# The first token and all weights in one DMA queue: reordering the start of a top-2 mixture-of-experts combine

## The chip, the core and the metric

The kernel runs on one core of a Trainium2 chip. The metric is the device time of one execution in microseconds (us), the median of three runs. The engines that matter here are VectorE (DVE in the profile), ScalarE (ACT), SyncE (SP), which computes nothing and issues transfers, and the core's 16 DMA engines, which move all data between device memory (DRAM) and the on-chip memory (SBUF, 128 partitions). SyncE and ScalarE each have a queue of their own for transfers; in the profile q1 is SyncE's and q10 is ScalarE's.

## The reference

```python
batch, seq, hidden, n_experts, k = 16, 1024, 512, 8, 2
# expert_outputs:  (16, 1024, 2, 512) float32
# combine_weights: (16, 1024, 2)      float32
def reference(expert_outputs, combine_weights):
    weights = combine_weights[..., np.newaxis]
    return np.sum(expert_outputs * weights, axis=2).astype(np.float32)
```

For each of the 16384 tokens two expert vectors of 512 elements are scaled by two weights and added. In float32 the input is 67.1 MB, the weights are 0.13 MB and the output is 33.6 MB, so 100.8 MB cross between DRAM and SBUF. There are two multiplications and an addition for every output element, and no matmul.

## The kernel before

A token here is a row of 2 x 512 float32 numbers, 4 KB long. Each of the 128 partitions handles 128 tokens: 120 in ten tiles of 12 tokens and 8 in a last, smaller tile. A full tile is 128 partitions x 48 KB, 6.29 MB. Four buffers hold tiles.

```python
J, LAST = 12, 8
main = per - LAST          # 120 tokens per partition in full tiles
...
ipool = ctx.enter_context(tc.tile_pool(name="in", bufs=4))
wt = wpool.tile([P, per * k], dt)

for t, c in ((0, main), (main, LAST)):          # weights: two DMAs in ScalarE's queue
    nc.scalar.dma_start(
        out=wt[:, k * t : k * (t + c)].rearrange("p (t k) -> p t k", k=k), in_=cw(t, c)
    )
warm = wpool.tile([P, 1], dt)
nc.scalar.activation(out=warm, in_=..., func=copy)
```

The two weight transfers have rows of 960 B and of 64 B per partition. The first serves the ten full tiles, the second the last tile only. The activation called `warm` loads ScalarE's function table early.

```python
for g in range(last + 1):
    et = ipool.tile([P, J, k * h], dt)
    ot = ...                                     # the first half of et, reused for the result
    t0, c = g * J, J if g < last else LAST

    for a, m in ((0, 2), (2, c - 2)) if g == 0 else ((0, c),):
        nc.sync.dma_start(
            out=et[:, a : a + m], in_=eo(t0 + a, m),
            max_dma_last_dim=k * h * 4 if g + a == 0 else None,
        )
    if g < last - 1:                             # tiles 0 to 8: VectorE alone
        ...
        nc.vector.tensor_tensor(out=ek, in0=ek, in1=wb, op=mult)                          # L78
        nc.vector.tensor_tensor(out=ot, in0=et[:, :, 0:h], in1=et[:, :, h : 2 * h], op=add)  # L79
        nc.scalar.dma_start(out=o(t0, c), in_=ot)
        continue
    ...                                          # tiles 9 and 10: ScalarE scales one half, VectorE does the rest
    nc.sync.dma_start(out=o(t0, c), in_=ot[:, 0:c])
```

The load of tile 0 is in two pieces: the first two tokens in rows of 4 KB (1024 KB in all), and then the other ten (5120 KB, rows of 40 KB). Every other tile is one load. VectorE's first multiply (L78) works on the whole of tile 0 at once. Loads stand in SyncE's queue; the stores of tiles 0 to 8 stand in ScalarE's, those of tiles 9 and 10 in SyncE's. A load into a buffer that was used before waits until the store from it has finished, so from tile 4 on loads and stores follow one another.

Of the kernel before, what the change touches and what calls it, by code (L numbers as in the profile page):

```python
# [1 line left out]

# [4 lines left out]


@with_exitstack
def kernel(  # L10
    ctx: ExitStack,
    tc: tile.TileContext,
    expert_outputs: bass.AP,
    combine_weights: bass.AP,
    out: bass.AP,
):

    nc = tc.nc  # L20
    b, s, k, h = expert_outputs.shape
    assert k == 2
    n = b * s
    P = nc.NUM_PARTITIONS
    per = n // P
    assert per * P == n
    J, LAST = 12, 8
    main = per - LAST
    assert main % J == 0
    eo = expert_outputs.rearrange("b s k h -> (b s) (k h)")  # L30
    cw = combine_weights.rearrange("b s k -> (b s) k")
    o = out.rearrange("b s h -> (b s) h")

    def rows(x):

        a = x[0 : P * main, :].rearrange("(p t) f -> p t f", p=P)
        b = x[P * main : n, :].rearrange("(p t) f -> p t f", p=P)
        return lambda t, c: a[:, t : t + c, :] if t < main else b[:, t - main : t - main + c, :]

    eo, cw, o = rows(eo), rows(cw), rows(o)  # L40

    dt = mybir.dt.float32
    mult = mybir.AluOpType.mult
    add = mybir.AluOpType.add
    copy = mybir.ActivationFunctionType.Copy

    last = main // J

    wpool = ctx.enter_context(tc.tile_pool(name="w", bufs=1))
    ipool = ctx.enter_context(tc.tile_pool(name="in", bufs=4))  # L50

    wt = wpool.tile([P, per * k], dt)

    for t, c in ((0, main), (main, LAST)):
        nc.scalar.dma_start(
            out=wt[:, k * t : k * (t + c)].rearrange("p (t k) -> p t k", k=k), in_=cw(t, c)
        )

    warm = wpool.tile([P, 1], dt)
    nc.scalar.activation(out=warm, in_=nc.const_aps.tensor(1.0, (P, 1), dt), func=copy)  # L60

    for g in range(last + 1):
        et = ipool.tile([P, J, k * h], dt)

        ot = et.rearrange("p j f -> p (j f)")[:, 0 : J * h].rearrange("p (j f) -> p j f", f=h)
        t0, c = g * J, J if g < last else LAST

        for a, m in ((0, 2), (2, c - 2)) if g == 0 else ((0, c),):
            nc.sync.dma_start(  # L69
                out=et[:, a : a + m],  # L70
                in_=eo(t0 + a, m),
                max_dma_last_dim=k * h * 4 if g + a == 0 else None,
            )
        if g < last - 1:

            wb = wt[:, g * J * k : (g + 1) * J * k].unsqueeze(2).to_broadcast([P, J * k, h])
            ek = et.rearrange("p j (k h) -> p (j k) h", k=k)
# [6 lines that stand above are left out]
        for i in range(c):  # L84
            t = t0 + i
            nc.scalar.activation(  # L86
                out=et[:, i, 0:h], in_=et[:, i, 0:h], func=copy, scale=wt[:, 2 * t : 2 * t + 1]
            )
            if g == last:
                nc.vector.scalar_tensor_tensor(  # L90
                    out=ot[:, i, :],
                    in0=et[:, i, h : 2 * h],
                    scalar=wt[:, 2 * t + 1 : 2 * t + 2],
                    in1=et[:, i, 0:h],
                    op0=mult,
                    op1=add,
                )
        if g < last:
            w1 = wt.rearrange("p (t k) -> p t k", k=k)[:, t0 : t0 + c, 1:2]
            x1 = et[:, :, h : 2 * h]  # L100
            nc.vector.tensor_tensor(out=x1, in0=x1, in1=w1.to_broadcast([P, c, h]), op=mult)  # L101
            nc.vector.tensor_tensor(out=ot, in0=et[:, :, 0:h], in1=x1, op=add)  # L102
        nc.sync.dma_start(out=o(t0, c), in_=ot[:, 0:c])


# [1 line left out]
_INS = ['expert_outputs', 'combine_weights']  # L107
_OUTS = [((16, 1024, 512), 'float32')]


# [23 lines left out]
```

## Time and profile before

| Quantity | Before |
|---|---|
| Device time, median of 3 runs | 239.06 us (238.92 to 240.28) |
| Span of the profiled execution | 237.3 us |
| VectorE busy | 193.9 us, 28 instructions |
| ScalarE busy | 14.0 us, 22 instructions |
| DRAM read, written | 67.24 MB, 33.55 MB |
| Multiply of one tile on VectorE | 12.96 us |
| Addition of one tile on VectorE | 6.56 us |
| Load of a full tile, issue to landing (median) | 29.9 us |
| Store of a full tile through ScalarE's queue, issue to landing (median) | 32.7 us |

The span is measured by the profiler on the core and is a little shorter than the device time. "Issue to landing" counts from the moment at which an engine issues a transfer until its completion is signalled; much of it is time in which the transfer shares the DMA engines with others or stands behind them. A line such as L78 is a line of the kernel's source. In the list of groups, the last part of a row tells how long the engine stood idle just before instructions of this group, and what ended the wait.

### The profile page before, as it was taken

Reading aid. Unit: us, or ns where it says so; the run is one execution under the profiler, and the core shown is the slowest. Engines: PE = TensorE matmul, PEld = TensorE weight load, DVE = VectorE, ACT = ScalarE, POOL = GpSimd, SP = SyncE. Lnnn points to the kernel's source line nnn. Section 1 sums busy time; section 2 is a strip of 40 time slices with the busy share of each in tenths; the row PEclk is TensorE's granted clock in tenths of the full one; section 3 lists DMA queues with packets and bytes.
Section 4 is the critical chain, followed back from the end, with each engine's and each line's share of the span. In section 5 each row is a group of like instructions: output and inputs, shape, how many; then the busy total and the mean of one; then the engine's idle time right before and its main releaser. Section 6 shows DMA issues by size and latency. Waiting matters only on the chain.

```text
span 237.3 us, 154 instructions
## 1 busy us (share of the span) xinstructions
DVE 193.9 (82%) x28; ACT 14.0 (6%) x22; POOL 0.2 (0%) x4
## 2 busy tenths in 40 slices
DVE  0008999999999999999999879969996998785710
ACT  2000000000000000000000000000000000740800
POOL 0000000000000000000000000000000000000000
DMA  8999999989899999999897999999997979999997
GB/s 308 443 456 406 398 431 497 398 356 505 356 439 435 427 464 464 398 398 522 348 522 344 452 427 435 464 464 398 398 522 340 530 336 460 458 403 442 402 438 309
DMA packets 3728, 100.80 MB, mean 425 GB/s; under 512 B 528, under 2 KB 656, under 8 KB 912
## 3 DMA queue, kind: packets, MB, share of 16 engines
q1 hardware_dynamic: 2144, 72.35, 71.1%
q10 hardware_dynamic: 1584, 28.44, 27.9%
HBM read 67.24 MB, written 33.55 MB: 425 GB/s over the span
## 4 chain that ended last, share of the span: by engine, by line
DMA 59%; DVE 33%; ACT 2%; DVEq 0%; ACTq 0%; issue 0%; SPq 0%
DMA et<-in_expert_outputs_dram 30%; DMA out_dram<-et 29%; DVE et L78 22%; DVE et L79 11%; ACT et L86 2%; DVE et L90 1%; DVEq L129 0%; ACTq L129 0%; SPq L69 0%; DVEq L78 0%; ACTq L86 0%
## 5 line engine op out<-in xcount | busy, mean ns | idle before, releaser
L78 DVE TENSOR_TENSOR et<-et,wt 128x12288 f32<-128x12288 f32 x9 | 116.6, 12955 | 25.2 <-DMA et<-in_expert_outputs_dram 25.2
L79 DVE TENSOR_TENSOR et<-et 128x6144 f32<-128x6144 f32 x9 | 59.0, 6558 | 0.3
L86 ACT ACTIVATE et<-et,wt 128x512 f32<-128x512 f32 x20 | 12.5, 707 | 209.2 <-DMA et<-in_expert_outputs_dram 209.2
L90 DVE SCALAR_TENSOR_TENSOR et<-et,wt 128x512 f32<-128x512 f32 x8 | 5.6, 748 | 3.9 <-ACT et L86 3.7
L101 DVE TENSOR_TENSOR et<-et,wt 128x6144 f32<-128x6144 f32 x1 | 6.6, 6559 | 2.3 <-DMA et<-in_expert_outputs_dram 2.3
L102 DVE TENSOR_TENSOR et<-et 128x6144 f32<-128x6144 f32 x1 | 6.6, 6559 | 0.9 <-ACT et L86 0.9
L60 ACT ACT_TABLE_LOAD x1 | 1.3, 1283 | 1.7 <-issue 1.7
L60 ACT ACTIVATE warm<-const-float32-1.0 128x1 f32<-128x1 f32 x1 | 0.2, 202 | 0.0
L118 POOL MEMSET const-bfloat16-1.0<- 128x1 bf16 x1 | 0.1, 102 | 0.0
L118 POOL MEMSET const-uint8-127<- 128x1 uint8 x1 | 0.1, 102 | 0.0
L118 POOL MEMSET const-float32-0.0<- 128x1 f32 x1 | 0.1, 99 | 0.2 <-issue 0.2
L118 POOL MEMSET const-float32-1.0<- 128x1 f32 x1 | 0.1, 99 | 0.0
## 6 DMA issues: line engine op xcount, KB each, us to landing
et<-in_expert_outputs_dram SPq DMA_DIRECT2D x9, 6144.0 KB, 29.9
out_dram<-et ACTq DMA_DIRECT2D x9, 3072.0 KB, 32.7
et<-in_expert_outputs_dram SPq DMA_DIRECT2D x1, 5120.0 KB, 17.3
et<-in_expert_outputs_dram SPq DMA_DIRECT2D x1, 4096.0 KB, 25.1
out_dram<-et SPq DMA_DIRECT2D x1, 3072.0 KB, 14.6
out_dram<-et SPq DMA_DIRECT2D x1, 2048.0 KB, 10.0
et<-in_expert_outputs_dram SPq DMA_DIRECT2D x1, 1024.0 KB, 5.4
wt<-in_combine_weights_dram ACTq DMA_DIRECT2D x1, 120.0 KB, 4.4
```

The costliest lines, as they stand in the source:

```text
L60: nc.scalar.activation(out=warm, in_=nc.const_aps.tensor(1.0, (P, 1), dt), func=copy)
L78: nc.vector.tensor_tensor(out=ek, in0=ek, in1=wb, op=mult)
L79: nc.vector.tensor_tensor(out=ot, in0=et[:, :, 0:h], in1=et[:, :, h : 2 * h], op=add)
L86: nc.scalar.activation(out=et[:, i, 0:h], in_=et[:, i, 0:h], func=copy, scale=wt[:, 2 * t : 2 * t + 1])
L90: nc.vector.scalar_tensor_tensor(out=ot[:, i, :], in0=et[:, i, h : 2 * h], scalar=wt[:, 2 * t + 1 : 2 * t + 2], in1=et[:, i, 0:h], op0=mul ...
L101: nc.vector.tensor_tensor(out=x1, in0=x1, in1=w1.to_broadcast([P, c, h]), op=mult)
L102: nc.vector.tensor_tensor(out=ot, in0=et[:, :, 0:h], in1=x1, op=add)
L118: nc = _bacc.Bacc("TRN2", target_bir_lowering=False, num_devices=1)
```

## The change

The start is rearranged, and nothing else is. Before, the weights were issued by ScalarE while SyncE issued the first two tokens as one transfer and then the rest of tile 0. After, SyncE issues all of them, one behind another in one queue: the first token, the weights of the full tiles, the weights of the last tile, the second token, and the other ten tokens of tile 0. Each of the two single tokens is one DMA with rows of 4 KB per partition, so the option that cut rows to 4 KB isn't needed any more.

The aim is an orderly start: a large transfer is first in line, the small weight rows come right behind it, and none of them takes turns with tile data from another queue. ScalarE issues no load any more, and its `warm` activation stands at the head of its program.

```diff
-    for t, c in ((0, main), (main, LAST)):
-        nc.scalar.dma_start(
+    warm = wpool.tile([P, 1], dt)
+    nc.scalar.activation(out=warm, in_=nc.const_aps.tensor(1.0, (P, 1), dt), func=copy)
+
+    def load_weights(t, c):
+        nc.sync.dma_start(
             out=wt[:, k * t : k * (t + c)].rearrange("p (t k) -> p t k", k=k), in_=cw(t, c)
         )
-
-    warm = wpool.tile([P, 1], dt)
-    nc.scalar.activation(out=warm, in_=nc.const_aps.tensor(1.0, (P, 1), dt), func=copy)
 
     for g in range(last + 1):
         ...
+        if g == 0:
 
-        for a, m in ((0, 2), (2, c - 2)) if g == 0 else ((0, c),):
-            nc.sync.dma_start(
-                out=et[:, a : a + m],
-                in_=eo(t0 + a, m),
-                max_dma_last_dim=k * h * 4 if g + a == 0 else None,
-            )
+            nc.sync.dma_start(out=et[:, 0:1], in_=eo(0, 1))
+            load_weights(0, main)
+            load_weights(main, LAST)
+            nc.sync.dma_start(out=et[:, 1:2], in_=eo(1, 1))
+        a = 2 if g == 0 else 0
+        nc.sync.dma_start(out=et[:, a:c], in_=eo(t0 + a, c - a))
```

## The prediction, made before the changed kernel had run

> **What bounds the kernel now.** I read the profile from the whole to the detail: the span in slices with the queue table under it, the chain that ended last, the groups of instructions, then the DMA issues and short windows at the start.
>
> The page's busy rows come first. DMA is the busy share of the 16 DMA engines in 40 slices of 5.93 us each (237.3 / 40), GB/s is what they moved; the queue table gives each queue's share of 16 engines over the whole span (q1 is filled by SyncE, q10 by ScalarE).
>
> ```profile
> DVE  0008999999999999999999879969996998785710
> ACT  2000000000000000000000000000000000740800
> ...
> DMA  8999999989899999999897999999997979999997
> GB/s 308 443 456 406 398 431 497 398 356 505 356 439 435 427 464 464 398 398 522 348 522 344 452 427 435 464 464 398 398 522 340 530 336 460 458 403 442 402 438 309
> DMA packets 3728, 100.80 MB, mean 425 GB/s; under 512 B 528, under 2 KB 656, under 8 KB 912
> ...
> q1 hardware_dynamic: 2144, 72.35, 71.1%
> q10 hardware_dynamic: 1584, 28.44, 27.9%
> ```
>
> The two queues together keep the DMA engines busy for 71.1 + 27.9 = 99.0% of the span: 0.99 x 237.3 = 234.9 us of transfer work and 2.4 us without. While busy they move 100.80 MB / 234.9 us = 429 GB/s. VectorE (DVE) is the only other engine with much to do, 193.9 us or 82%. So the kernel is bound by transfers from end to end, and whatever leaves bytes and packets alone can only touch the 2.4 us.
>
> The chain that ended last agrees, if read with care: 59% of it is DMA, 33% DVE. The DVE part lies mostly in 18.6 to 77.1 and 137.7 to 157.2 us, and transfers ran on beside it: in the slices of these two stretches the DMA row has no digit under 8. The groups of instructions show VectorE's slack: it waits for a load in several places, not the transfers for it.
>
> ```profile
> L78 DVE TENSOR_TENSOR et<-et,wt 128x12288 f32<-128x12288 f32 x9 | 116.6, 12955 | 25.2 <-DMA et<-in_expert_outputs_dram 25.2
> ```
>
> Of these 25.2 us of idle time 18.6 are the wait for the first tile; the rest is three waits of 2.15 to 2.21 us before tiles 6 to 8 (the timeline of DVE). So VectorE catches up with the loads in mid-kernel, and an earlier or later first multiply by a microsecond or two ends in a longer or shorter wait there.
>
> Now the stage that the change touches. Windows at the start (us, then busy us and count of each engine, clock, DMA share, GB/s):
>
> ```profile
> 0.00:1.80 1.80, 0.00 (x0) 0.06 (x1) 0.20 (x4) 1.00 0.00 0
> 1.80:3.20 1.40, 0.00 (x0) 1.39 (x2) 0.00 (x0) 1.00 0.98 228
> 3.20:5.20 2.00, 0.00 (x0) 0.03 (x1) 0.00 (x0) 1.00 1.13 439
> 5.20:18.50 13.30, 0.00 (x0) 0.00 (x0) 0.00 (x0) 1.00 1.05 452
> ```
>
> No packet moves before 1.8 us; then 1.4 us at 228 GB/s, and full rate after that. The slow stretch moves 0.32 MB where 429 GB/s would move 0.60 MB, a loss of (0.60 - 0.32) / 0.429 = 0.65 us. The start thus costs 1.8 + 0.65 = about 2.4 us of transfer time, most of it before any packet. (A packet's bytes are booked in one moment, so shares over 1 occur and short windows are good to some tenths.)
>
> The issues say which transfers those are; the last number is the us from issue to landing:
>
> ```profile
> et<-in_expert_outputs_dram SPq DMA_DIRECT2D x1, 5120.0 KB, 17.3
> ...
> et<-in_expert_outputs_dram SPq DMA_DIRECT2D x1, 1024.0 KB, 5.4
> wt<-in_combine_weights_dram ACTq DMA_DIRECT2D x1, 120.0 KB, 4.4
> wt<-in_combine_weights_dram ACTq DMA_DIRECT2D x1, 8.0 KB, 17.1
> ```
>
> The 8 KB of weights for the last tile take 17.1 us, as long as the 5 MB of tile 0: its small packets take turns with large ones. Nothing before the last tile waits for them.
>
> **What the Trainium skill says.** "DMA: Bandwidth & Descriptors", section "Queues, rings and completion order": each DMA engine goes round its queues packet by packet. The 17.1 us above agree. Section "Issuing engines are not separate DMA queues": transfers issued by different engines run on the same 16 DMA engines, and a second issuer saves issue time only. The trace agrees: the two shares add to 99%, not to more. Section "Where 436 GB/s comes from" gives a ceiling of 435 GB/s; an estimate from it for this kernel's bytes is 100.80 / 0.435 = 231.7 us, and the trace's 429 GB/s while busy is within 1.5% of that.
>
> **The change, part by part.**
>
> 1. *Weights leave ScalarE's queue.* This takes away two issues of 0.43 and 0.51 us on ScalarE (timeline). ScalarE then waits until 203 us for its next input, so this is worth nothing.
>
> 2. *The weights' packets go into SyncE's queue.* The same 256 rows (960 B and 64 B long) are moved. In a window over 0 to 19 us they make q10 288 packets and 2.4% of 16 engines: 0.024 x 19 = 0.46 us of transfer work. It is paid before and after. They now stand in line ahead of the second token instead of taking turns: no change in the sum.
>
> 3. *The first load of 1024 KB becomes two of 512 KB*, both with 4 KB rows: 256 such packets either way. One more transfer means 16 more small packets: of the 528 under 512 B, 128 are the 64 B rows, and the other 400 are 16 for each of the 25 transfers (12 loads, 2 of weights, 11 stores). Their bytes are nothing. In all I expect 3744 packets, q1 2144 + 288 + 16 = 2448 and q10 1584 - 288 = 1296.
>
> 4. *SyncE issues more in a row before the bulk.* Before, five issues took 2.62 us, 0.52 us each. After, the fifth one is the bulk of tile 0, which before was the second, at 1.22 us: it starts at about 0.73 + 4 x 0.52 = 2.8 us. Does the queue run dry? From issue to first packet took 1.8 - 0.73 = 1.07 us. So first token at 1.8, weights ready at 2.3 and 2.85, second token at 3.4, bulk at 3.9 us. The first token's 0.52 MB take 0.52 / 0.429 = 1.2 us at full rate, plus the 0.65 us that the slow stretch cost before: until 3.0 at the earliest, 3.7 us likely. The weights add 0.46: 3.5 to 4.1 us. The second token is ready at 3.4 us, just in time; it lasts to 4.7 or 5.3 us, and the bulk is ready 0.8 us ahead of that. So no gap; at worst some tenths.
>
> 5. *Tile 0 complete.* VectorE's first multiply waits for the weights and all of tile 0. The same 6.42 MB stand ahead of the end of tile 0, so it starts at 18.3 to 18.9 us (18.64 before).
>
> 6. *One wait is new.* In the built program the load of tile 3 now waits for a completion counter used by the first token, reused because there is one transfer more. The first token lands at about 4 to 5 us, and behind it tiles 0 to 2 are queued, 18.9 MB or 44 us of transfers. It costs nothing. All other waits are the same in kind: a load waits for the store that frees its buffer.
>
> Sum: 0 from parts 1, 2, 5 and 6; 0 to +0.4 us from part 4; up to -0.3 us if the slow stretch shrinks because the two queues no longer take turns in it. Middle: +0.05 us. From 239.06 us this gives 239.1 us.
>
> **Rivals.**
>
> *A, starvation:* issues in one queue are slower than 0.52 us each or the weights' rows hold up the line, and DMA engines stand idle before the bulk arrives. For it: the margin in part 4 is tenths of a microsecond, and one of the five issues before took 0.67 us. Against it: the 0.46 us for all weight packets. With twice the spacing the bulk would come at 0.73 + 4 x 1.04 + 1.07 = 6.0 us, the data end at about 5.3, and it would cost 0.7 us, plus a gap of about a microsecond ahead of the second token: 240.5 us at most.
>
> *B, a real gain at the start:* tile 0 lands earlier and the whole program moves forward. The slow stretch has 0.65 us, so 238.4 us at best. Against it: its packets and its first-packet latency stay.
>
> *C, VectorE's earlier or later start changes which loads and stores overlap, and so the end.* At the end the last load lands at 219.85 us, VectorE needs until 226.5 us (start of the last store), and the store before lands at 217.04 + 14.6 = 231.6 us: through all this the DMA engines have work. The overlap would have to shift by over 5 us for a gap there. This is hidden: 239 us.
>
> *D, weights as the new wait ahead of the first multiply:* they were at 5 us, and must now come after 18 us to matter. No.
>
> **Range and chances.** The three runs before lie between 238.92 and 240.28 us, a spread larger than any part above. B gives 238.4 and A 240.5 us as unlikely ends; I take 238.3 to 240.0 us. 2% is 4.8 us, twice all the time that the DMA engines don't work; a gain of that size is closed off, and a loss of that size needs a cause that I don't see: 1% and 2%, and 97% for within 2%.
>
> **What would show it.** Packets 3744, the queues 2448 and 1296, total busy share still 99%, mean 424 to 426 GB/s; SyncE's fifth issue at 2.6 to 3.1 us; both weight transfers landing by 6 us (before 5.1 and 18.3); the first multiply at 18.3 to 18.9 us; three waits of VectorE near 2 us in mid-kernel; span within 1 us of 237.3. I would be wrong if windows between 3 and 6 us showed DMA shares far under 1 (A), or if the mean rate over 20 to 220 us changed from 430 GB/s, which nothing in the change explains.

## The result, and the profile after

The changed kernel takes 240.81 us (240.51 to 241.5) where the kernel before took 239.03 us. The ratio is 1.0064, with a 95% interval of 1.0039 to 1.0090: slower by about 1.5 us, within 2%, but outside the range of 238.3 to 240.0 us. (Here and below the ratio comes from all executions, which spread over more than a microsecond; it isn't the quotient of the two medians.) The span grew from 237.3 to 239.0 us.

The page of the changed kernel: DMA busy share and GB/s in 40 slices (5.98 us each now), packets, and the two queues.

```profile
DMA  7999999999999999999999999999999999999996
GB/s 232 418 433 444 444 420 428 387 424 457 424 411 448 428 461 428 436 436 420 428 453 407 424 432 457 444 436 420 444 436 420 444 411 428 437 422 435 436 420 261
DMA packets 3744, 100.80 MB, mean 422 GB/s; under 512 B 544, under 2 KB 672, under 8 KB 928
...
q1 hardware_dynamic: 2448, 72.48, 71.1%
q10 hardware_dynamic: 1296, 28.31, 27.5%
```

The packet counts are the predicted ones. In the middle nothing is lost: from 20 to 220 us the mean rate is 432 GB/s, 430 before. The weak slices are the first (232 GB/s, 308 before) and the last (261, 309 before). First the start, in the windows used before, and SyncE's issues (start us, us, line, transfer, count; rows with a count above 1 join neighbouring issues):

```profile
0.00:1.80 1.80, 0.00 (x0) 1.08 (x1) 0.20 (x4) 1.00 0.08 14
1.80:3.20 1.40, 0.00 (x0) 0.41 (x2) 0.00 (x0) 1.00 0.85 219
3.20:5.20 2.00, 0.00 (x0) 0.00 (x0) 0.00 (x0) 1.00 1.04 328
5.20:18.50 13.30, 0.00 (x0) 0.00 (x0) 0.00 (x0) 1.00 1.05 435
```

```profile
0.73 0.38 SPq L69 DMA_DIRECT2D et<-in_expert_outputs_dram  x1
1.16 0.90 SPq L58 DMA_DIRECT2D wt<-in_combine_weights_dram  x2
2.10 0.43 SPq L72 DMA_DIRECT2D et<-in_expert_outputs_dram  x1
2.58 194.11 SPq L74 DMA_DIRECT2D et<-in_expert_outputs_dram  x11
```

Between 3.2 and 5.2 us the rate is 328 GB/s instead of 439, and behind 5.2 us it is 435 against 452. The busy share of 1.04 doesn't mean that no engine stood idle: this view books a packet's whole time and all its bytes at the moment at which it starts. Worked out from the packets in the two traces, with each one spread over its own time, the rates are 313 GB/s (399 before) from 3.2 to 5.2 us, 358 (430 before) from 5.2 to 8 us and 434 (433 before) from 14 to 30 us. Up to 14 us, on the mean of the 16 engines:

- the engines stand idle for about 0.2 us more than before;
- the packets of the first two tokens take 0.26 us longer in all;
- the packets of the last piece of tile 0, its other ten tokens, take 0.46 us longer in all: up to 2.82 us for one of them, where each took 1.51 or 1.52 us in the kernel before.

The first multiply starts at 19.77 us instead of 18.64 us.

Now the end, in windows of half a microsecond: first the kernel before, then the changed one. Rows as above; only the last number, GB/s, is needed.

```profile
235.00:235.50 0.50, 0.00 (x0) 0.00 (x0) 0.00 (x0) 1.00 1.15 492
235.50:236.00 0.50, 0.00 (x0) 0.00 (x0) 0.00 (x0) 1.00 0.09 33
236.00:236.50 0.50, 0.00 (x0) 0.00 (x0) 0.00 (x0) 1.00 0.01 0
```

```profile
235.00:235.50 0.50, 0.00 (x0) 0.00 (x0) 0.00 (x0) 1.00 1.15 492
235.50:236.00 0.50, 0.00 (x0) 0.00 (x0) 0.00 (x0) 1.00 0.92 393
236.00:236.50 0.50, 0.00 (x0) 0.00 (x0) 0.00 (x0) 1.00 0.69 295
236.50:237.00 0.50, 0.00 (x0) 0.00 (x0) 0.00 (x0) 1.00 0.39 164
237.00:237.50 0.50, 0.00 (x0) 0.00 (x0) 0.00 (x0) 1.00 0.16 66
```

The last store has rows of 16 KB, and one such packet in half a microsecond is 16.4 KB / 0.5 us = 33 GB/s. Each takes 0.61 us and is booked where it starts, so these numbers count the engines that start another packet: before, one of them does so after 235.5 us; after, 12, 9, 5 and 2 do in successive windows. By the trace's packets the 16 engines end between 235.72 and 236.18 us before, and between 236.03 and 237.79 us after. Two quantities come out of this view, and the experiments are read by them:

- **Bytes left at 235.0 us**: (492 + 33) x 0.5 = 262 KB before, (492 + 393 + 295 + 164 + 66) x 0.5 = 705 KB after. They are in packets that start after that time. The difference of 443 KB is 1.03 us at 429 GB/s. This is how far the engines are behind on the mean of the 16.
- **The tail**: how long single engines go on after the others. The rest of the 1.7 us of span is here. The last store is complete when the slowest engine is, 1.61 us later than before.

### The profile page after: what moved, and what is told of

It reads as the page before. It is cut to its first block, busy times and chain, and to the rows that moved or that the text cites. A ratio compares the mean times of both kernels' runs of the same rounds, so it can differ in the third digit from the quotient of the medians.

```text
span 239.0 us, 157 instructions
## 1 busy us (share of the span) xinstructions
DVE 194.0 (81%) x28; ACT 14.0 (6%) x22; POOL 0.2 (0%) x4
## 2 busy tenths in 40 slices
DMA packets 3744, 100.80 MB, mean 422 GB/s; under 512 B 544, under 2 KB 672, under 8 KB 928
## 3 DMA queue, kind: packets, MB, share of 16 engines
q1 hardware_dynamic: 2448, 72.48, 71.1%
## 4 chain that ended last, share of the span: by engine, by line
DMA 59%; DVE 33%; ACT 2%; SPq 1%; DVEq 0%; issue 0%; ACTq 0%
DMA et<-in_expert_outputs_dram 30%; DMA out_dram<-et 29%; DVE et L79 22%; DVE et L80 11%; ACT et L87 2%; DVE et L91 1%; SPq L58 0%; DVEq L130 0%; ACTq L130 0%; SPq L72 0%; SPq L69 0%; DVEq L79 0%; SPq L74 0%; ACTq L87 0%
```

## The experiments

In all of them "weights" means both weight loads, "bulk" the last piece of tile 0. The runs of the kernel before beside them had medians from 239.06 to 239.16 us. Its executions fall into two groups: of 202, 143 took 238.92 to 239.4 us, and 59 took 239.5 us or more, up to 241.0 us. A median therefore says little without the shortest execution beside it, and a profile shows one execution only.

### First four: which part costs

**The split only**, weights back in ScalarE's queue (there behind the table load):

```diff
-        nc.sync.dma_start(      # in load_weights
+        nc.scalar.dma_start(
```

> The changed kernel with both weight loads back in ScalarE's queue; the first two tokens stay split into two loads. Theory 1 (small rows in line: 16 small weight rows per DMA engine stand in the same queue ahead of tile data, and the reads behind them start cold again): 239.0 us, as before the change, and tile 0 complete near 18.5 us. Theory 2 (late issue: the second token and the bulk are issued too late, behind the two weight loads): also near 239.0 us. Theory 3 (the split itself: two loads of one token are slower than one of two): 240.5 to 240.8 us, as after the change.

Measured: 240.19 us (238.97 to 241.08), ratio 1.0028 (1.0012 to 1.0045). 312 KB were left at 235.0 us, only 0.1 us more than before, in an execution of 240.96 us. Its last windows:

```profile
235.00:235.50 0.50, 0.00 (x0) 0.00 (x0) 0.00 (x0) 1.00 1.15 492
235.50:236.00 0.50, 0.00 (x0) 0.00 (x0) 0.00 (x0) 1.00 0.09 33
236.00:236.50 0.50, 0.00 (x0) 0.00 (x0) 0.00 (x0) 1.00 0.08 33
236.50:237.00 0.50, 0.00 (x0) 0.00 (x0) 0.00 (x0) 1.00 0.08 33
237.00:237.50 0.50, 0.00 (x0) 0.00 (x0) 0.00 (x0) 1.00 0.08 33
```

One engine of 16 works alone for two microseconds. Its fifteen neighbours finished as in the kernel before. So the total has two terms, and no theory had the second.

**Weights behind the bulk**, all in SyncE's queue:

```diff
+            # token, token, bulk, then:
+            load_weights(0, main)
+            load_weights(main, LAST)
```

> All in SyncE's queue as after the change, but both weight loads stand behind the bulk of tile 0, so that they come up only at about 17 us, long after everything has been issued. Theory 1 (small rows in line): the slow stretch moves to about 17 us, behind the weight rows; total still 240.3 to 240.8 us. Theory 2 (late issue): nothing is late any more; 239.0 us. Theory 3 (split): 240.5 to 240.8 us with the slow stretch still at 4 to 7 us.

Measured: 239.07 us, ratio 0.9999 (0.9987 to 1.0011); 262 KB left. The loss is gone. The same weight rows, in the same queue behind the same split, cost nothing at 17 us. Theory 1 in its plain form falls, and so does theory 3 as the cause of the lost bytes. Theory 2 stands so far: in this order the bulk is also issued earlier, at 1.62 us instead of 2.58.

**Two tokens joined** ahead of the weights:

```diff
-            nc.sync.dma_start(out=et[:, 0:1], in_=eo(0, 1))
+            nc.sync.dma_start(out=et[:, 0:2], in_=eo(0, 2), max_dma_last_dim=k * h * 4)
             load_weights(0, main)
             load_weights(main, LAST)
-            nc.sync.dma_start(out=et[:, 1:2], in_=eo(1, 1))
```

> The first two tokens as one load of 1024 KB, then both weight loads, then the bulk, all in SyncE's queue. With 1024 KB ahead, the DMA engines have data until about 5 us, by when the bulk has long been issued. Theory 1 (small rows in line): 240.3 to 240.8 us, with slow first packets of the bulk. Theory 2 (late issue): 239.0 to 239.3 us. Theory 3 (split): 239.0 us.

Measured: 240.01 us, ratio 1.0033 (1.0022 to 1.0043); 360 KB left, 0.2 us behind. More data ahead of the weights takes most of the lost bytes away, but the bulk, issued at 2.2 us and needed about 5.3 us, still came slowly. Theory 2 as stated wanted less.

**No weights** (the result is not weighted):

```diff
+    nc.gpsimd.memset(wt, 0.5)
...
-            load_weights(0, main)
-            load_weights(main, LAST)
```

> The changed kernel without its two weight loads (the weights are filled with a constant on chip, so the weighting of the result is left out). Theory 1 and theory 2: the loss goes, and with it 0.46 us of weight transfers: 238.4 to 238.7 us. Theory 3 (split): the loss stays, 240.1 to 240.4 us.

Measured: 238.64 us, ratio 0.9992 (0.9973 to 1.0011), with 33 KB left, 0.53 us ahead of the kernel before. The 0.46 us that the weights' packets cost by the prediction agree with this and with the medians, which are 0.44 us apart; the loss of the change is gone with them.

### Four more: rate, count and position

**Four tokens first** (2048 KB), then the weights:

```diff
-            nc.sync.dma_start(out=et[:, 0:1], in_=eo(0, 1))
+            nc.sync.dma_start(out=et[:, 0:4], in_=eo(0, 4))
             ...            # weights, then et[:, 4:12]
```

> In SyncE's queue: four tokens as one load (2048 KB, rows of 16 KB), both weight loads, then the other eight tokens. The weights stand at the same depth in issues as in the run with two joined tokens, but 2048 KB ahead of them last until about 7 us instead of 5. Theory A (rows become ready at a limited rate, some 0.9 us for each transfer of 128 rows in one queue, whatever their length; small rows are used up faster than that): everything is ready by then, 239.0 us or a little less, since longer first rows also shorten the slow stretch at the start. Theory B (whatever stands behind the small weight rows starts cold): 240.0 us or more, as with the two joined tokens.

Measured: 239.88 us (238.92 to 240.56), ratio 1.0008 (0.9991 to 1.0025); the profiled execution took 238.97 us, with 262 KB left. In this execution no bytes are lost when the weights come up at 7 us. But it is one of the short ones: 14 of the 22 took 239.5 us or more, and none of those was profiled. The expected 239.0 us came in 7 of the 22.

**Weights twice:**

```diff
             load_weights(0, main)
             load_weights(main, LAST)
+            load_weights(0, main, w2)
+            load_weights(main, LAST, w2)
```

> The changed kernel with each weight load issued twice in SyncE's queue (the second copies go to a tile that nothing reads). The added transfer work is 0.46 us. Theory A (0.9 us for each transfer to become ready): the second token is ready two transfers later, 1.8 us; 242.3 to 242.8 us. Theory B (a cold start once behind the small rows): 241.2 to 241.4 us, the added work alone. Theory C (only SyncE's issue spacing of 0.47 us counts): about 241.7 us.

Measured: 241.46 us, ratio 1.0094 (1.0075 to 1.0113); 852 KB left. Two more transfers ahead of the second token add 0.65 us to the changed kernel, not 1.8. Theory A's fixed time for each transfer falls; most of the 0.65 us is the 0.46 us of work, and theory B's 241.2 to 241.4 us come nearest.

**Only the 64 B rows between the tokens**, the 960 B rows behind the bulk:

```diff
-            load_weights(0, main)
             load_weights(main, LAST)
             ...            # second token, bulk
+            load_weights(0, main)
```

> The changed kernel with only the 64 B rows (8 KB in all) between the two tokens; the 960 B rows (120 KB) stand behind the bulk of tile 0. Theory A (a limited rate of transfers becoming ready): one transfer less ahead of the second token; the loss against before shrinks by about half, to 239.6 to 240.1 us, though hardly a byte is left in between. Theory B (cold start behind small rows): 240.4 to 240.8 us, as after the change. A theory by bytes: 239.1 us.

Measured: 240.17 us, ratio 1.0040 (1.0025 to 1.0055); 540 KB left, 0.65 us behind. The last windows show most of the engines late, not one or two:

```profile
235.00:235.50 0.50, 0.00 (x0) 0.00 (x0) 0.00 (x0) 1.00 0.76 328
235.50:236.00 0.50, 0.00 (x0) 0.00 (x0) 0.00 (x0) 1.00 0.92 393
236.00:236.50 0.50, 0.00 (x0) 0.00 (x0) 0.00 (x0) 1.00 0.84 360
236.50:237.00 0.50, 0.00 (x0) 0.00 (x0) 0.00 (x0) 1.00 0.01 0
```

8 KB in line do most of the damage of 128 KB. It isn't the bytes. The slow stretch came later than in the changed kernel. With each packet spread over its own time the rates are 363 GB/s from 3.2 to 5.2 us and 325 GB/s from 5.2 to 8 us, when the bulk was due; its packets took up to 2.64 us.

**The split alone**, weights first in ScalarE's queue as before the change:

```diff
-        for a, m in ((0, 2), (2, c - 2)) if g == 0 else ((0, c),):
+        for a, m in ((0, 1), (1, 1), (2, c - 2)) if g == 0 else ((0, c),):
```

> The kernel before, with nothing changed but the first two tokens as two loads of one token; the weights stay in ScalarE's queue and stay first there (in the run with the split only, they came behind ScalarE's table load). Theories A and B: 239.0 to 239.1 us. Theory 3 (the split itself costs): 240.2 us or more. If this is 239.1 us, the slower executions of that earlier run come from the late weights in ScalarE's queue, and not from the split.

Measured: 240.20 us (238.97 to 240.99), ratio 1.0027 (1.0009 to 1.0044). Profiled in an execution of 239.04 us: 262 KB left, as before. The late weights in ScalarE's queue were thus not the reason of the first run's slower executions.

### Four at the start of the queue

**The same sequence later**, at the head of tile 1:

```diff
+            nc.sync.dma_start(out=et, in_=eo(0, J))          # tile 0 whole
+            e1 = new_tile()                                  # tile 1: token, weights, token, bulk
```

> The very sequence of the change (token, 960 B rows, 64 B rows, token, ten tokens), but at the head of tile 1, behind the whole of tile 0 as one load: it comes up at about 16.5 us instead of 1.8 us, when all of it was issued more than 10 us before. Theory A or any other by which something is not ready in the first microseconds: no loss, 238.7 to 239.1 us. Theory B, by which the sequence itself makes the reads behind it slow: a loss of about 1 us at 17 to 21 us, 240.0 us or more. Some executions may be 1 us slower with either, as those before the change are.

Measured: 239.16 us (238.97 to 239.79), ratio 0.9997 (0.9987 to 1.0007); 278 KB left. At this place the sequence costs nothing, and theory B falls. It costs where it stands in the first microseconds.

**Tile 0 whole**, then the weights, as a candidate:

```diff
+            nc.sync.dma_start(out=et, in_=eo(0, J))
             load_weights(0, main)
             load_weights(main, LAST)
```

> A candidate: tile 0 as one load with rows of 48 KB at the head of SyncE's queue, both weight loads behind it, then tile 1. Nothing small stands in the first 16 us. Theory A: no loss, and a shorter slow stretch at the start, 238.6 to 239.0 us. Theory B: a cold start behind the weights at about 17 us, 240 us.

Measured: 239.95 us, ratio 1.0019 (1.0007 to 1.0032). 312 KB left, and a tail of two engines (66 GB/s in the window from 236.0 us; they end at 236.82 and 236.93 us, the others by 236.14). Not a gain: longer first rows did not shorten the start, and a tail came that neither theory had. It was the rule here: 20 of the 22 executions took 239.5 us or more.

**Two joined tokens with rows of 8 KB:**

```diff
-            nc.sync.dma_start(out=et[:, 0:2], in_=eo(0, 2), max_dma_last_dim=k * h * 4)
+            nc.sync.dma_start(out=et[:, 0:2], in_=eo(0, 2))
```

> As the run with the two joined tokens, but their load has rows of 8 KB (128 rows) instead of 4 KB (256 rows); the same bytes stand ahead of the weights. If rows become ready at a limited rate (theory A), 128 rows less ahead of the bulk make it ready about 0.9 us earlier and the loss of that run (0.93 us) is gone: 239.0 to 239.3 us. If only the time since the start or the bytes ahead count, it stays near 240.0 us.

Measured: 239.70 us, ratio 1.0010 (0.9994 to 1.0026); 377 KB left, 0.3 us behind, no better than the 360 KB with 4 KB rows. Half the rows did not make the bulk ready sooner: its packets took 0.50 us longer in all than in the kernel before, on the mean of the engines, against 0.20 us with 4 KB rows. So theory A's count of rows falls too. The total lies between the two expectations and decides nothing.

**Half tokens**, with no weight rows in this queue:

```diff
+            for i in (0, 1):
+                for f in (0, h):
+                    nc.sync.dma_start(out=et[:, i : i + 1, f : f + h], in_=eo(i, 1)[:, :, f : f + h])
```

> The kernel before, with the weights first in ScalarE's queue, but the first two tokens in SyncE's queue as four loads of half a token (256 KB each, rows of 2 KB, 0.6 us of data each), then the bulk as the fifth transfer, issued at about 2.6 us as in the changed kernel. No tiny rows stand in this queue. If short transfers in a row are the cause, whatever they hold (theory A): the bulk is late by some tenths to 1 us, 239.5 to 240.5 us, with low rates at 4 to 7 us. If it takes rows as tiny as those of the weights: 239.1 us.

Measured: 240.56 us, ratio 1.0046 (1.0031 to 1.0060); 508 KB left, 0.57 us behind. A part of this is work: a packet of 2 KB took 0.084 us where one of 4 KB takes 0.159, which makes about 0.14 us for these 512 packets on the mean of the engines. The bulk's packets took up to 1.99 us. So weight rows in this queue are not needed for the loss: short transfers of tile data at its head do it as well.

### Issue time alone

Short transfers also delay the issue of what follows. Three runs hold the bulk back by a fill on GpSimd in its buffer, with the two tokens ahead of it and the weights in ScalarE's queue:

```diff
+        if g == 0:
+            nc.gpsimd.memset(et[:, 2:6].rearrange("p j f -> p (j f)")[:, 0:1400], 0.0)   # 2000, 2800
```

> The kernel before with two loads of one token, weights in ScalarE's queue; the bulk of tile 0 stays the third transfer in SyncE's queue but is held back by a fill of 1400 elements on GpSimd in its buffer, so that SyncE issues it at about 2.1 us instead of 1.64 us, as in the run with the 64 B rows alone in line (where it was the fourth transfer, and about 0.9 us were lost). Nothing short is added to the queue. Theory L1 (time from issue to full rate, over 2.5 us and under load more): low rates appear at 5 to 8 us, 239.5 to 240.2 us. Theory L2 (the short transfers ahead of it in the queue hold it up, not its issue time): no low rates, 239.0 us, apart from single slower executions as with the split alone.

> The same with a fill of 2000 elements: bulk issued at about 2.6 us, as in the changed kernel. L1: 0.5 us more than with 1400 elements, 240.0 to 240.7 us. L2: still 239.0 us and full rate at 5 to 8 us.

> The same with a fill of 2800 elements: bulk issued at about 3.3 us. L1: 0.7 us more again, 240.7 to 241.4 us. L2: the first packets of a transfer came 1.0 us after its issue at the start, and data last until 5.2 us: none or at most some tenths lost, 239.0 to 239.4 us.

Measured: 240.09, 240.60 and 240.81 us, ratios 1.0025 (1.0008 to 1.0042), 1.0040 (1.0022 to 1.0058) and 1.0051 (1.0032 to 1.0069). SyncE issued the bulk at 2.02, 2.52 and 3.19 us. The totals are L1's. Its mechanism hardly shows in the profiles: from 5.2 to 8 us, with each packet spread over its own time, the rates are 414, 419 and 424 GB/s (429 with the split alone, 358 in the changed kernel), and 312, 312 and 328 KB are left. But the second profiled execution was the shortest of its kernel, so three more executions were profiled.

> The bulk held to 2.5 us once more, for the profile of another execution: the one profiled first took 239.4 us and was the shortest of its kernel (median 240.6 us). If this one takes 240.4 us or more, L1 expects all engines late: 0.5 us or more of bytes more than before left at 235.0 us (0.48 MB or more in all, against 0.26 MB before), with a low rate at 5 to 8 us. L2 with single engines behind expects at most 0.35 MB left at 235.0 us, and one to four engines still at work after 236.0 us, 33 GB/s each.

> The bulk held to 3.2 us once more, for another execution's profile. The same reading: L1 expects 0.5 MB or more left at 235.0 us; L2 with single engines behind expects at most 0.35 MB, and one to four engines at work after 236.0 us.

> The split alone once more, for another execution's profile: the one profiled first took 239.0 us, the median is 240.2 us. If this one takes 240.4 us or more, single engines behind (expected here, since the issue is as early as before the change) show as 33 to 66 GB/s after 236.0 us with no more than 0.35 MB left at 235.0 us; a cause that slows all engines would leave 0.5 MB or more.

They took 240.14, 240.72 and 240.87 us and left 344, 377 and 312 KB. In the last microseconds, the bulk held to 3.2 us and then the split alone:

```profile
235.50:236.00 0.50, 0.00 (x0) 0.00 (x0) 0.00 (x0) 1.00 0.32 131
236.00:236.50 0.50, 0.00 (x0) 0.00 (x0) 0.00 (x0) 1.00 0.15 66
236.50:237.00 0.50, 0.00 (x0) 0.00 (x0) 0.00 (x0) 1.00 0.00 0
237.00:237.50 0.50, 0.00 (x0) 0.00 (x0) 0.00 (x0) 1.00 0.08 33
```

```profile
235.50:236.00 0.50, 0.00 (x0) 0.00 (x0) 0.00 (x0) 1.00 0.02 0
236.00:236.50 0.50, 0.00 (x0) 0.00 (x0) 0.00 (x0) 1.00 0.08 33
236.50:237.00 0.50, 0.00 (x0) 0.00 (x0) 0.00 (x0) 1.00 0.08 33
237.00:237.50 0.50, 0.00 (x0) 0.00 (x0) 0.00 (x0) 1.00 0.08 33
```

With the bulk at 3.2 us the bytes left amount to 0.27 us on the mean of the engines (377 KB, a little over what L2 allowed and well under L1's 0.5 MB), and they belong to four engines: twelve ended by 235.95 us, as in the kernel before, and the last at 237.65 us. With the split alone it is one engine (237.88 us, the others by 235.96). So in these profiles a late issue costs mostly through single engines that fall behind, not through a low rate of all; the short transfers ahead in the queue cost both.

In the total, though, the late issue is nearly as dear. The changed kernel issues its bulk at 2.58 us and has a median of 240.81 us; with the bulk held to 2.52 us and nothing short in line it is 240.60 us. What the short transfers add is that no execution gets away: the shortest took 240.51 us in the changed kernel (of six executions), 239.44 us with the bulk held to 2.52 us, and 238.92 us before the change.

## Why the prediction was wrong, by its own steps

**What bounds the kernel: right, with one blind spot.** Transfers bind it from end to end. VectorE's waits in mid-kernel are as long as before, with a short one more (0.32, 2.22, 2.14 and 2.23 us where there were 2.17, 2.21 and 2.15), because the loads moved back with it: the first multiply is 1.13 us later, that of tile 6 already 1.60 us (139.26 against 137.66). The 99% are a mean over 16 engines. In the run with the split only, the late engine carried its last three packets alone while the other fifteen had finished, so no other engine took over its share; and as the engines have work all the time (a busy share of 1.00 from 20 to 220 us), an engine that starts late finds no gap in which to catch up. The slowest one sets each landing and the end, and a mean share can't show it.

**Part 1 (ScalarE): right.** ScalarE had nothing to do with the time that it gained.

**Part 2 (weights in SyncE's queue): the work right, the conclusion wrong.** The 0.46 us are there with or without the change, as the run without weights shows. "No change in the sum" failed: what stands behind these rows at the start came slowly.

**Part 3 (packets): right**, 3744, 2448 and 1296.

**Part 4 is the step that failed: "So no gap; at worst some tenths."** The issue times were good: the bulk was predicted at 2.8 us and came at 2.58 us. The step from there to "no gap" was not: the 1.07 us from issue to first packet, taken from the first transfer in an empty queue, were applied to every transfer, and full speed was assumed from its first packet on. The run with the 64 B rows only has its bulk issued at 2.09 us and needed about 5 us, nearly 3 us later, and yet 0.65 us were lost. In place of "some tenths" the changed kernel lost 1.03 us on the mean of its engines and 1.61 us on the slowest, most of it in packets that took longer and about 0.2 us in idle engines.

**Part 5: wrong with part 4.** The first multiply was at 19.77 us, not 18.3 to 18.9.

**Part 6 (the new wait): right.** SyncE waited 15.3 us for loads in all, 15.2 before; nothing stood still for it. Both weight transfers landed by 5.1 us (1.16 + 3.7 and 1.64 + 3.4), as predicted.

**Rivals.** A had the right place and nearly the size (240.5 us "at most"), and its reason was right in small part: issues were 0.47 us apart, not slower, and the DMA engines were idle for only about 0.2 us of the loss; most of it was slow packets. Its sign, shares "far under 1", could not come, as this view books a slow packet's whole time at its start. B's gain did not come: the stretch from 1.8 to 3.2 us stayed at 219 GB/s (228 before). C was right that loads and stores leave no gap at the end; the tail of single engines is something else. D was right.

**What the runs show as the cause.** Two things. First, short transfers ahead of tile data in the same queue, within the first 5 us, put most of the engines behind: with 128 KB of weights, with 8 KB, and with half tokens and no weights in that queue. A bulk held back as long, with nothing short ahead of it, does this only in small part (312 to 377 KB left, against 705). The lost bytes shrink with 1024 KB ahead of the short transfers, and are gone behind the bulk, 15 us later, and, in the one execution profiled, with 2048 KB ahead. They grew from one short transfer to two (0.65 and 1.03 us), but not from two to four beyond the added work (0.34 us for 0.46). Second, single engines finish late. This sets the total of the slower executions, and it comes more often when the bulk is issued late: 29 of 32 executions took 239.5 us or more with the bulk held to 2.5 or 3.2 us, 28 of 44 with the split alone.

**Open.** How the DMA engines come to be slow behind the short transfers isn't shown; two proposals (a fixed time for each transfer, a rate by rows) fell. Nor is it shown why single engines fall behind: 59 of 202 executions of the kernel before take 239.5 us or more as well. The split alone doesn't explain it. With it, 28 of 44 executions were that long when the weights came through ScalarE's queue, but 2 of 13 when they stood behind the bulk in SyncE's. No version tried was faster than the kernel before; weights behind the bulk equals it, all in one queue.

## What to carry to other kernels

Where transfers bind, read the last microseconds in short windows: the staircase of GB/s counts how many DMA engines still start packets, which a busy share of 99% hides, and a delay of the first microseconds is still there 230 us later. At the head of a queue put large data, issue it early, and let small loads come after it. With all loads in one queue, two of the orders tried here kept the time of the kernel before: the two tokens, the bulk and then the weights (239.07 us), and tile 0 whole with the weights between the tokens of tile 1 (239.16 us). It is no guarantee: tile 0 whole with the weights right behind it took 239.95 us. The time from issue to first packet in an empty queue is no measure for a transfer that stands fourth in line.

## What was not expected of the hardware

- One DMA engine of 16 can end about 2 us after the others, and the whole kernel waits for it (33 GB/s for four windows in the run with the split only; it ended at 237.97 us, the others by 236.02).
- A busy share of 1.04 went with 328 GB/s. Near the start packets of 4 KB took up to 0.98 us, where most took 0.16 us, and rows of 40 KB up to 2.82 us where 1.51 us is usual. So a busy share must be read with the rate.
- Rows of 48 KB, 16 KB, 8 KB or 4 KB at the head of the queue made little difference to the start (1.1 to 1.2 MB moved by 5.2 us, each packet spread over its own time); tile 0 as a single load, simplest of all, ended 0.2% later than the kernel before.
